# A hybrid attention block on one Trainium2 core: staged queries stored over ScalarE's queue, the second half's weights requested first, its norms moved beside the keys, the first norm weight spread by TensorE

## The chip, the cores and the metric

The kernel runs on one NeuronCore of a Trainium2 chip. TensorE multiplies matrices and transposes tiles (its weight loads are shown as PEld and overlap its matmuls), VectorE (DVE), ScalarE (ACT) and GpSimd (POOL) do the elementwise work, and DMA engines move data between DRAM and the on-chip memory. DMAs are issued by an instruction in some engine's own stream; in this kernel nearly all of them are issued by SyncE (SP), which does nothing else. An engine works through its instructions strictly in order: one that waits for a semaphore holds up everything behind it, DMA issues included. The metric is the device time of one execution in microseconds, given as the median of several executions; the kernel is also run once with the hardware profiler, and this one execution is what the views show.

## The reference, cut to what matters

One transformer block over 1024 tokens of width 1024, batch 1, in float32. The kernel keeps float32 accuracy.

```python
def reference(x, mem, ...):
    for l in range(DEPTH):                                   # DEPTH = 1
        x = x + _hybrid_mixer(_rms_norm(x, norm1_g[l]), w_in[l], ...)
        x = x + _memory_xattn(_rms_norm(x, norm2_g[l]), mem, ...)
        x = x + _sq_relu_mlp(_rms_norm(x, norm3_g[l]), ...)
...
    # in _hybrid_mixer; proj is 1024 tokens x 1760 columns
    proj = h @ w_in
    c_q, c_kv, k_idx, w_idx, q_nsa, kv_nsa, g_nsa = jnp.split(proj, splits, axis=-1)
    c_q = _rms_norm(c_q, dsa_cq_g)
    q_d = _rope(_rms_norm((c_q @ w_dsa_uq).reshape(B, L, DSA_HEADS, D), dsa_qn_g), pos)
    q_i = _rope((c_q @ w_idx_q).reshape(B, L, IDX_HEADS, IDX_DIM), pos)
    q_n = _rope(_rms_norm(q_nsa.reshape(B, L, NSA_HEADS, D), nsa_qn_g), pos)
    # per block of 128 queries: index scores and top 256 keys, an attention over those,
    # and compressed, selected and windowed attentions, mixed by gates; then o @ w_out
```

Three kinds of queries come out of the projection: `q_d` (kind 0, 8 heads of 64), `q_n` (kind 1, 8 heads) and `q_i` (kind 2, 8 heads, for the index scores). Kinds 0 and 1 are normalised per head and rotated; kind 2 is rotated only.

## The kernel before

**The projection** (`project`, L385) runs twice, for two halves (parts) of four tiles of 128 tokens each. Part 0 runs alone at the start. Part 1 runs as the first piece of a generator `fill` (driver, from L1224), and `together` interleaves `fill` with `attend`, the attention of the eight query blocks. The rest of `fill` is the keys and values of the memory (`memory`, L886), the output projection and memory attention of pairs of tiles (`between`, L929), and the first half of the MLP (`mlp`, L1059). What is left of the MLP follows by itself at the end (`mlp_tail`, L1117). The text order decides only which work is offered: a list scheduler then fixes the order of the instructions on each engine, so a few moved lines can reorder much.

**Each part** goes through these steps. The four tiles of `x` are normalised and transposed to xh (and xl in part 0). In part 0 this is `norm_T` (L293): a square with a row sum on ACT, a power on POOL (L238), a scaling by the norm weight `gb1` on DVE (L298), eight transposes on TensorE (`to_T`, L285), and evacuations by ACT and DVE (L289, L291, or L242 and L243). For part 1 the tiles have been normalised in place before, by `norm_ahead` (L375: square L380 on ACT, scaling L382 on DVE, with the norm weight loaded by `gain`, L353), so that part 1 begins with the transposes alone. Then `w_in` runs as chunks of columns, in the order (968,256), (0,256), (256,200)+(1736,24), (1224,256), (1480,256), then the small `w_dsa_ukv`, then (456,256), (712,256) beside the keys' preparation `k_prep` (L483), and at last the four gemms "ups" (`w_dsa_uq` and `w_idx_q`, two chunks of 256 columns each). In the part 0 of before, `norm_ahead` runs beside the ups.

**Weights** come in groups of two (KG) slabs of 128 rows. In part 0, `load_w` (L258, DMA L261 on SP) loads them and `split_w` splits them in a high and a low part (L251 on ACT, L256 on POOL or DVE). In part 1, `load_whole` (L268, DMA L272 on SP) loads them into the rings `whi` and `wlo` and they are used as plain float32. `mm` is L222-223, so all matmuls of the gemms show that line; their outputs go to the PSUM tile `psD`.

**The queries** are put aside in DRAM: `stage_q` (L426) copies each `psD` tile of 128x256 to an on-chip tile `st` (L430 on DVE for the tiles with t % 2 == part unless it is kind 1, else L432 on ACT), and after the fourth tile one DMA (L434, 512 KB, on SP) stores `st` to the DRAM tensor `qraw`. There are six such stores in each part. SP thus holds, in one order, the stores, the loads of the weights, and the loads of the queries below.

**The attention** reads queries back in `q_prep` (L586), four heads at a time: a load `qin` from `qraw` (L590, on SP, one buffer), for kinds 0 and 1 two small products of the rotation tables with the norm weight into `qtab` (L597, L598 on POOL, one buffer), the square (L600, ACT), the sum and power (L602 to L604), the scaling of `qin` (L605), the products `qta` (L606, POOL) and `qtb` (L607, DVE), the sums into the two halves of `qd` (L609 on DVE, L610 on POOL, one buffer), four transposes into `psPT` (L616), and the split into qh and ql (L242, L243). The queries are prepared 44 times, 32 of them with tables.

**The start.** `x`'s first tile is loaded first (L229, SP). `gb1`, the norm weight on all 128 partitions, is loaded by a broadcast DMA of 512 KB on ACT's queue (L392). The first weights (L261) and the other tiles (L373) follow on SP, then the tables (L199), small norm weights (L1234 to L1236), masks (L205) and the small loads of `project` into `pc` (L412 to L415, L422).

**DMA semaphores.** The DMAs issued by SP take eight semaphores in turn, so a DMA's issue also waits until the one eight before it has landed.

Of the kernel before, what the change touches and what calls it, by code (L numbers as in the profile page):

```python
# [9 lines left out]
F32 = mybir.dt.float32  # L10
# [6 lines left out]
AF = mybir.ActivationFunctionType  # L17
# [5 lines left out]
P = 128  # L23
L = 1024
DM = 1024
# [121 lines left out]
def alternate(*streams):  # L147
    streams = list(streams)
    i = 0
    while streams:  # L150
        i %= len(streams)
        w = next(streams[i], None)
        if w is None:
            streams.pop(i)
        else:
            i += 1
            yield w
# [12 lines left out]
def build(nc, tc, I, C, out):  # L170
    v, s, g, te = nc.vector, nc.scalar, nc.gpsimd, nc.tensor
    ctx = ExitStack()
    W = {n: I[n][0] for n in I}
# [12 lines left out]
    def pst(tag, shape):  # L186
        return psum["pool"].tile(shape, F32, tag=tag, name="ps" + tag, bufs=psum["n"][tag],
                                 padded_shape=[P, 512 // int(np.prod(shape[2:]))] + list(shape[2:]))
# [5 lines left out]
    def row(ap):  # L194
        return ap[None, :]
# [26 lines left out]
    def mm(o, a, b, start, stop):  # L222
        te.matmul(o, a, b, start=start, stop=stop)  # L223

    def small(pool, tag, w, dt=F32, bufs=2, p=P):
        return pool.tile([p, w], dt, tag=tag, name=tag, bufs=bufs)
# [66 lines left out]
    def norm_T(pool, x_t, gb, xs):  # L293
        ss = small(at, "nss", 1)
        xn = ring(pool, "x4", [P, DM])
        s.activation(xn, x_t, AF.Square, accum_out=ss)
        r = rsqrt_of(at, ss, DM, 1, "n")
        v.scalar_tensor_tensor(xn, x_t, r[:, 0:1], gb, op0=ALU.mult, op1=ALU.mult)  # L298
        to_T(pool, xn, xs, DM // P)
# [70 lines left out]
    ahead = {0: late["x"]}  # L370
# [4 lines left out]
    def norm_ahead(pool):  # L375

        gb = gain(pool, W["norm1_g"])
        for t in range(4, 8):
            ss = small(at, "nss", 1)
            s.activation(ring(pool, "x4", [P, DM]), ahead[t], AF.Square, accum_out=ss)  # L380
            r = rsqrt_of(at, ss, DM, 1, "n")
            v.scalar_tensor_tensor(ahead[t], ahead[t], r[:, 0:1], gb, op0=ALU.mult, op1=ALU.mult)  # L382
            yield 1.0

    def project(pool, part, late, st):  # L385
        t0, nt = PARTS[part]
        whole = part > 0
        _, xf, xt_of = xT(pool, nt, whole)
        begun = []
        if not whole:  # L390
            gb1 = ring(pool, "x4", [P, DM])
            s.dma_start(gb1, row(W["norm1_g"]).to_broadcast([P, DM]))  # L392
            ws = weights(pool, xf, DM // P, W["w_in"], [(968, 256)])
            for t in range(1, nt):
                begun += [next(ws) for _ in range(KG)]
                ahead[t] = small(srow, "S", L, bufs=NS)
                load_x(ahead[t], t)
            begun += list(ws)
        for t in range(nt):
            if whole:  # L400
                to_T(pool, ahead.pop(t0 + t), xt_of(t), DM // P, True)
            else:
                norm_T(pool, ahead.pop(t), gb1, xt_of(t))
            yield 1.0
        pe = late["pe"]
        cq = [ring(pool, "c8", [P, nt, 2, P], F32 if whole else F32R) for _ in xf]
# [17 lines left out]
        qst = []  # L424

        def stage_q(k, c, t, pt):  # L426
            if t == 0:
                qst[:] = [ring(pool, "st", [P, nt, 256])]
            if k != 1 and t % 2 == part:
                v.tensor_copy(qst[0][:, t, :], pt)  # L430
            else:
                s.activation(qst[0][:, t, :], pt, AF.Copy)  # L432
            if t == nt - 1:
                nc.sync.dma_start(qraw[k][part][c], qst[0])  # L434

        def consume(ci, t, pt):
            T = t0 + t
# [38 lines left out]
        def w_in(chunks, first, begun=None):  # L476
            return gemm(pool, xf, DM // P, nt, W["w_in"], chunks,
                        lambda ci, t, pt: consume(ci + first, t, pt), begun)
# [36 lines left out]
        for kv in range(0 if part else 2):  # L515
# [6 lines left out]
        yield from (alternate if part == 0 else chain)(*pair_)  # L522
        yield from gemm(pool, [lambda t, k, c=c: c[:, t, :] for c in ckv], 1, nt,
                        W["w_dsa_ukv"], [[(0, 128)]], consume_kv)
        yield from alternate(w_in([[(456, 256)], [(712, 256)]], 2), k_prep())
        ups = chain(*[gemm(pool, [lambda t, k, c=c: c[:, t, k, :] for c in cq], 2, nt,
                           W[name], [[(0, 256)], [(256, 256)]],
                           lambda ci, t, pt, k=k: stage_q(k, ci, t, pt)) for k, name in ((0, "w_dsa_uq"), (2, "w_idx_q"))])
        yield from ups if whole else alternate(ups, norm_ahead(pool))

    def compress(pool, part, KT, pe, st, ctab):
        t0, nt = PARTS[part]
# [52 lines left out]

    def q_prep(aw, t, kind, hg):  # L586

        q = small(aw, "qin", 256, bufs=1).rearrange("p (h d) -> p h d", d=64)
        part = part_of(t)
        nc.sync.dma_start(q, qraw[kind][part][hg][:, t - PARTS[part][0], :].rearrange("p (h d) -> p h d", d=64))  # L590
        ta = small(aw, "qta", 256, bufs=1).rearrange("p (h d) -> p h d", d=64)
        tb = small(aw, "qtb", 256, bufs=1).rearrange("p (h d) -> p h d", d=64)
        if kind == 2:
            A, B = cos[:, t, None, None, :].to_broadcast([P, 4, 2, 32]), sin[:, t, :]
        else:
            tab = small(aw, "qtab", 128, bufs=1).rearrange("p (a d) -> p a d", d=64)
            g.tensor_tensor(halves(tab[:, 0, :]), halves(qg[:, kind, :]), cos[:, t, None, :].to_broadcast([P, 2, 32]), op=ALU.mult)  # L597
            g.tensor_tensor(tab[:, 1, :], sin[:, t, :], qgs[:, kind, :], op=ALU.mult)  # L598
            A, B = halves(tab[:, 0, :])[:, None, :, :].to_broadcast([P, 4, 2, 32]), tab[:, 1, :]
            s.activation(ta, q, AF.Square)  # L600
            ss, r = small(aw, "qss", 4), small(aw, "qr", 4)
            v.tensor_reduce(ss, ta, axis=AX.X, op=ALU.add)  # L602
            g.tensor_scalar(ss, ss, 64 * EPS, None, op0=ALU.add)
            g.tensor_tensor(r, ss, mhalf[:, 0:1].to_broadcast([P, 4]), op=ALU.pow)  # L604
            g.tensor_tensor(q, q, r[:, :, None].to_broadcast([P, 4, 64]), op=ALU.mult)  # L605
        g.tensor_tensor(halves(ta), halves(q), A, op=ALU.mult)  # L606
        v.tensor_tensor(halves(tb), swap(q), halves(B)[:, None, :, :].to_broadcast([P, 4, 2, 32]), op=ALU.mult)  # L607
        qd = small(aw, "qd", 512, bufs=1).rearrange("p (h b d) -> p h b d", h=4, b=2)
        v.tensor_tensor(qd[:, :, 0, :], ta, tb, op=ALU.add)  # L609
        g.tensor_tensor(qd[:, :, 1, :], ta, tb, op=ALU.add)  # L610
        own = ("iqh", "iql", 1) if kind == 2 else ("qh", "ql", 2)
        qh = aw.tile([P, 4, P], F32R, tag=own[0], name=own[0], bufs=own[2])
        ql = aw.tile([P, 4, P], F32R, tag=own[1], name=own[1], bufs=own[2])
        p2 = pst("PT", [P, 4, P])
        for h in range(4):
            te.transpose(p2[:, h, :], qd[:, h, :, :].rearrange("p b d -> p (b d)"), ident)  # L616
        split_ps(p2, qh, ql)
        return qh, ql
# [633 lines left out]
    aw = aw_pool.__enter__()  # L1252
# [63 lines left out]
```

## Time and profile before

| | |
|---|---|
| median of 3 runs | 1768.23 us (1766.14 to 1768.61) |
| the profiled execution, its own time | 1767.5 us |
| its span in the profile | 1765.7 us |
| mean granted TensorE clock | 0.987 |
| TensorE busy | 1682.6 us, 95% of the span, 9326 matmuls |
| ACT, DVE, POOL busy | 1077.3, 953.5, 883.2 us |
| DMA | 188.03 MB, mean 106 GB/s |
| stores of staged queries (L434) | 12 of 512 KB, 2.9 us each from issue to landing |

How to read it: the span starts with the first instruction of the program, and 1.8 us of the execution lie outside it. Times in a row of the timeline are the start and the duration in us, then the engine, the line of the kernel, the operation, the tile written, the tiles read, the shape and the count; a bracket at the end gives the engine's idle time just before and what ended it. "SPq" marks time of SP's queue, waits included. A row of the waits gives the waiting engine and line, what released it, and then the total us, the number of waits and the longest one. A row of the windows gives for each engine the busy us and the count of instructions, then the TensorE clock that was granted, the share of the DMA engines' time, and GB/s. A row of the chain of waits gives the start, the duration and the work that the end waited for. In the groups and waits, L223 stands for every gemm and every attention matmul; the tile tells them apart.

### The profile page before, as it was taken

Reading aid. Unit: us, or ns where it says so; the run is one execution under the profiler, and the core shown is the slowest. Engines: PE = TensorE matmul, PEld = TensorE weight load, DVE = VectorE, ACT = ScalarE, POOL = GpSimd, SP = SyncE. Lnnn points to the kernel's source line nnn. Section 1 sums busy time; section 2 is a strip of 40 time slices with the busy share of each in tenths; the row PEclk is TensorE's granted clock in tenths of the full one; section 3 lists DMA queues with packets and bytes.
Section 4 is the critical chain, followed back from the end, with each engine's and each line's share of the span. In section 5 each row is a group of like instructions: output and inputs, shape, how many; then the busy total and the mean of one; then the engine's idle time right before and its main releaser. Section 6 shows DMA issues by size and latency. Waiting matters only on the chain.

```text
span 1765.7 us, 28018 instructions
## 1 busy us (share of the span) xinstructions
PE 1682.6 (95%) x9326; PEld 1446.5 (82%) x9326; DVE 953.5 (54%) x2398; ACT 1077.3 (61%) x2697; POOL 883.2 (50%) x1025
## 2 busy tenths in 40 slices
PE   6998999899998899999999999999999989999998
PEld 6997987788787778868888788888888978888887
DVE  4564668667774776545664556567645532222233
ACT  5443895995698558955599655897634533333333
POOL 2355465664442256757666667562313524444455
PEclk9998999999999899999999999999999989999999
DMA  7434312663343321222222212226257522333333
GB/s 204 128 122 115 80 51 86 205 172 111 95 146 108 96 60 58 77 77 70 65 67 70 88 59 65 66 95 202 78 187 230 162 66 89 95 96 95 96 120 108
DMA packets 173233, 188.03 MB, mean 106 GB/s; under 512 B 25248, under 2 KB 141728, under 8 KB 173088
## 3 DMA queue, kind: packets, MB, share of 16 engines
q1 hardware_dynamic: 165008, 175.22, 32.7%
q0 software_dynamic: 7936, 10.49, 2.2%
q8 instruction: 74, 1.21, 0.3%
q10 hardware_dynamic: 144, 0.52, 0.1%
q14 instruction: 71, 0.58, 0.1%
HBM read 168.36 MB, written 17.83 MB: 105 GB/s over the span
## 4 chain that ended last, share of the span: by engine, by line
PE 75%; DVE 7%; DMA 5%; ACT 5%; issue 4%; POOL 4%; SPq 1%; POOLq 0%; DVEq 0%; ACTq 0%
PE psD L223 54%; PE psS L223 8%; PE psPV L223 5%; PE psPT L729 4%; PE psM L285 1%; POOL wlo L256 1%; DMA wraw<-in_w_ff_in_dram 1%; PE psPT L616 1%; ACT dmask L670 1%; ACT S L714 1%; DVE S L712 1%; DVE pl L243 1%; POOL S L719 1%; DVE isc L644 0%; DMA whi<-in_w_out_dram 0%
## 5 line engine op out<-in xcount | busy, mean ns | idle before, releaser
L256 POOL TENSOR_TENSOR wlo<-wraw,whi 128x512 fp32r<-128x512 f32 (+1 forms) x225 | 306.8, 1369 | 289.8 <-ACT whi L251 287.8
L223 PE MATMUL psD<-whi,h 128*128 128x512 f32 x1024 | 338.6, 399 | 8.8 <-DVE b L1184 5.4
L251 ACT ACTIVATE whi<-wraw 128x512 fp32r<-128x512 f32 x321 | 200.3, 628 | 216.9 <-PE psD L223 157.4
L223 PEld LDWEIGHTS psD<-whi,h 128*128 128x128 f32 x1024 | 191.4, 189 | 54.1 <-DVE b L1184 8.8
L223 PE MATMUL psD<-xh,whi 128*128 128x512 f32 (+1 forms) x576 | 213.6, 374 | 0.9 <-ACT xh L242 0.7
L223 PE MATMUL psD<-xh,wlo 128*128 128x512 f32 (+1 forms) x576 | 213.2, 370 | 0.3 <-POOL wlo L256 0.3
L223 PE MATMUL psD<-xl,whi 128*128 128x512 f32 (+1 forms) x576 | 211.8, 369 | 0.0
L223 PE MATMUL psD<-wlo,h 128*128 128x512 f32 x512 | 203.2, 398 | 2.1 <-POOL wlo L256 2.0
L243 DVE TENSOR_TENSOR pl<-psPT,ph 128x512 fp32r<-128x512 f32 (+1 forms) x232 | 142.0, 620 | 69.1 <-ACT ph L242 67.4
L714 ACT ACTIVATE S<-S,mn 128x128 f32<-128x128 f32 (+7 forms) x192 | 142.7, 744 | 46.0 <-DVE mn L712 41.9
L223 PE MATMUL psD<-wlo,xh 128*128 128x256 f32 (+1 forms) x608 | 165.0, 348 | 0.8 <-DMA wlo<-in_w_in_dram 0.8
L223 PE MATMUL psD<-whi,xh 128*128 128x256 f32 (+1 forms) x608 | 163.3, 346 | 0.9 <-DVE Vd L243 0.9
L256 DVE TENSOR_TENSOR wlo<-wraw,whi 128x512 fp32r<-128x512 f32 (+1 forms) x96 | 78.9, 822 | 146.6 <-ACT whi L251 146.3
L242 ACT ACTIVATE ph<-psPT 128x512 fp32r<-128x512 f32 (+1 forms) x232 | 122.6, 540 | 52.7 <-PE psPT L729 45.9
L719 POOL TENSOR_SCALAR S<-S,sums,gi 128x640 f32<-128x640 f32 (+7 forms) x128 | 106.3, 839 | 87.8 <-DVE sums L717 66.1
L729 PE MATMUL psPT<-c_ident,S 128*128 128x128 f32 x816 | 131.3, 276 | 4.4 <-POOL S L719 4.0
L223 PEld LDWEIGHTS psD<-xh,wlo 128*128 128x128 f32 x576 | 108.8, 189 | 18.5 <-POOL wlo L256 1.6
L223 PEld LDWEIGHTS psD<-xh,whi 128*128 128x128 f32 x576 | 108.7, 189 | 18.2 <-ACT xh L242 1.1
L223 PEld LDWEIGHTS psD<-xl,whi 128*128 128x128 f32 x576 | 108.5, 189 | 17.4
L223 PEld LDWEIGHTS psD<-wlo,xh 128*128 128x128 f32 x608 | 114.2, 193 | 9.4 <-issue 0.9
L223 PEld LDWEIGHTS psD<-whi,xh 128*128 128x128 f32 x608 | 113.0, 192 | 9.5 <-DVE Vd L243 1.1
L223 PEld LDWEIGHTS psD<-wlo,h 128*128 128x128 f32 x512 | 96.5, 189 | 22.8 <-POOL wlo L256 5.0
(302 smaller groups left out, 3946.4 us busy)
## 6 DMA issues: line engine op xcount, KB each, us to landing
wraw<-in_w_ff_in_dram SPq DMA_DIRECT2D x40, 512.0 KB, 4.0
wraw<-in_w_ff_out_dram SPq DMA_DIRECT2D x40, 512.0 KB, 3.8
wraw<-in_w_ff_in_dram SPq DMA_DIRECT2D x64, 256.0 KB, 2.8
wraw<-in_w_ff_out_dram SPq DMA_DIRECT2D x64, 256.0 KB, 2.6
whi<-in_w_out_dram SPq DMA_DIRECT2D x32, 256.0 KB, 4.1
wlo<-in_w_out_dram SPq DMA_DIRECT2D x32, 256.0 KB, 4.1
wraw<-in_w_in_dram SPq DMA_DIRECT2D x24, 256.0 KB, 3.8
q<-st SPq DMA_DIRECT2D x12, 512.0 KB, 2.9
```

The lines of the kernel that those rows point to most:

```text
L223: te.matmul(o, a, b, start=start, stop=stop)
L242: s.activation(hi, src, AF.Copy)
L243: v.tensor_tensor(lo, src, hi, op=ALU.subtract)
L251: s.activation(hi, raw, AF.Copy)
L256: (v if l == "v" else g).tensor_tensor(lo, raw, hi, op=ALU.subtract)
L285: te.transpose(pt[:, j, :], x_t[:, (c + j) * P:(c + j + 1) * P], ident)
L616: te.transpose(p2[:, h, :], qd[:, h, :, :].rearrange("p b d -> p (b d)"), ident)
L670: s.activation(mask, src, AF.Sign, bias=c, accum_out=over)
L712: v.tensor_tensor_reduce(out=dst, in0=sp, in1=m, scale=1.0, scalar=mn[:, 0:1] if i else 3e38, op0=ALU.add, op1=ALU.min, accum_out=low)
L714: s.activation(S, S, AF.Exp, bias=low, scale=-1.0, accum_out=sums[:, hh:hh + 1])
L719: g.tensor_scalar(Ss[hh], Ss[hh], sums[:, hh:hh + 1], 1.0 if gate is None else gate[:, hh:hh + 1], op0=ALU.mult, op1=ALU.mult)
L729: te.transpose(p2[:, j, hh, :], S[:, (c + j) * P:(c + j + 1) * P], ident)
```

## The change

Six edits, all in `project` and `q_prep`:

1. The first norm weight is loaded as one row of 4 KB into partition 0 of `gb1` (still on ACT's queue); two matmuls with a row of ones as the stationary operand spread it over 128 partitions into two `psD` tiles of 128x512, and one copy on ACT and one on DVE put them into `gb1`. `norm_T`'s instructions are issued after both copies.
2. In part 1, the first chunk of `w_in` is requested at the head of the generator, ahead of the transposes.
3. `stage_q` stores over ACT's queue in place of SP's, and in both parts it is the even tiles that DVE copies.
4. `norm_ahead` runs beside the chunks (456,256), (712,256) and `k_prep` of part 0.
5. `q_prep`'s `qin` has two buffers (the default of `small`) in place of one, and the rotation tables lie in the first quarter of `qd` in place of a buffer of their own.
6. The ups of part 0 run without `norm_ahead` beside them.

```diff
-        begun = []
+        begun = list(weights(pool, xf, DM // P, W["w_in"], [(968, 256)])) if whole else []
         if not whole:
             gb1 = ring(pool, "x4", [P, DM])
-            s.dma_start(gb1, row(W["norm1_g"]).to_broadcast([P, DM]))
+            s.dma_start(gb1[0:1], row(W["norm1_g"]))
+            ones = pool.tile([1, P], F32, tag="ones", name="ones")
+            v.memset(ones, 1.0)
+            spread = []
+            for c in range(2):
+                spread.append(pst("D", [P, 512]))
+                mm(spread[c], ones, gb1[0:1, c * 512:(c + 1) * 512], True, True)
+            copies = [s.activation(gb1[:, 0:512], spread[0], AF.Copy), v.tensor_copy(gb1[:, 512:], spread[1])]
...
-                norm_T(pool, ahead.pop(t), gb1, xt_of(t))
+                with tc.issue_after(copies[0].ins), tc.issue_after(copies[1].ins):
+                    norm_T(pool, ahead.pop(t), gb1, xt_of(t))
...
-            if k != 1 and t % 2 == part:
+            if k != 1 and t % 2 == 0:
                 v.tensor_copy(qst[0][:, t, :], pt)
             else:
                 s.activation(qst[0][:, t, :], pt, AF.Copy)
             if t == nt - 1:
-                nc.sync.dma_start(qraw[k][part][c], qst[0])
+                s.dma_start(qraw[k][part][c], qst[0])
...
-        yield from alternate(w_in([[(456, 256)], [(712, 256)]], 2), k_prep())
+        yield from alternate(w_in([[(456, 256)], [(712, 256)]], 2), k_prep(), *([] if whole else [norm_ahead(pool)]))
...
-        yield from ups if whole else alternate(ups, norm_ahead(pool))
+        yield from ups
...
-        q = small(aw, "qin", 256, bufs=1).rearrange("p (h d) -> p h d", d=64)
+        q = small(aw, "qin", 256).rearrange("p (h d) -> p h d", d=64)
...
+        qd = small(aw, "qd", 512, bufs=1).rearrange("p (h b d) -> p h b d", h=4, b=2)
...
-            tab = small(aw, "qtab", 128, bufs=1).rearrange("p (a d) -> p a d", d=64)
+            tab = qd[:, 0, :, :]
...
-        qd = small(aw, "qd", 512, bufs=1).rearrange("p (h b d) -> p h b d", h=4, b=2)
```

## The prediction

> **What bounds the kernel now.** I read the page's engine totals first, then its chain, then the windows by stage, and only then the timelines of the stages with idle TensorE.
>
> ```profile
> PE 1682.6 (95%) x9326; PEld 1446.5 (82%) x9326; DVE 953.5 (54%) x2398; ACT 1077.3 (61%) x2697; POOL 883.2 (50%) x1025
> PE 75%; DVE 7%; DMA 5%; ACT 5%; issue 4%; POOL 4%; SPq 1%; POOLq 0%; DVEq 0%; ACTq 0%
> ```
>
> The first line is busy time by engine, the second the chain of waits by engine. TensorE works 95% of the span of 1765.7 us. The edits add two matmuls and take none away, so time can come only from the other 83 us (1765.7 - 1682.6) and from stretches where TensorE ran at a lower clock. The windows say where these lie:
>
> ```profile
> 0.00:25.00 25.00, 12.77 (x85) 11.62 (x86) 12.61 (x24) 12.12 (x21) 4.85 (x10) 1.00 0.67 217
> 75.00:100.00 25.00, 24.05 (x202) 23.87 (x201) 8.92 (x21) 10.01 (x31) 11.47 (x10) 1.00 0.55 179
> 100.00:125.00 25.00, 24.85 (x208) 24.54 (x208) 20.41 (x35) 13.87 (x32) 16.39 (x19) 1.00 0.39 146
> ...
> 130.00:140.00 10.00, 2.71 (x10) 1.91 (x11) 4.71 (x10) 1.99 (x4) 5.59 (x9) 0.71 0.61 147
> 140.00:150.00 10.00, 10.00 (x42) 8.51 (x41) 2.58 (x10) 2.53 (x8) 5.62 (x10) 0.78 0.96 228
> ...
> 310.00:335.00 25.00, 19.59 (x117) 15.53 (x118) 18.59 (x66) 23.12 (x74) 14.78 (x26) 1.00 0.68 218
> ...
> 500.00:650.00 150.00, 133.57 (x762) 116.64 (x760) 97.00 (x272) 108.55 (x286) 51.28 (x71) 0.94 0.36 106
> 650.00:1300.00 650.00, 637.89 (x3434) 537.62 (x3435) 384.43 (x920) 472.93 (x1073) 386.98 (x404) 1.00 0.27 82
> ```
>
> Four places are idle and lie near the edits: the start (12 us of the first 25), the seam between part 0 and part 1 (7.3 us of 130 to 140, with a granted clock of 0.71 and then 0.78), the seam between part 1 and the memory (5.4 us of 310 to 335), and the attention (16.4 us of 500 to 650, 12.1 of 650 to 1300). The seam at 130 is where three of the edits point, so I read it closely. TensorE there:
>
> ```profile
> 125.19 0.28 PE L223 MATMUL psD<-whi,c 128*128 128x256 f32 x1
> ...
> 128.53 1.04 PE L285 MATMUL psD<-c_ident,S 128*128 128x128 f32 x8
> 132.00 0.66 PE L285 MATMUL psM<-c_ident,S 128*128 128x128 f32 x4 [2.43 <-ACT xh L289]
> 136.44 1.11 PE L616 MATMUL psPT<-c_ident,qd 128*128 128x128 f32 x4 [3.79 <-POOL qd L610]
> ...
> 139.48 3.75 PE L223 MATMUL psD<-wlo,xh 128*128 128x256 f32 x8 [0.82 <-DMA wlo<-in_w_in_dram]
> ...
> 143.52 1.54 PE L223 MATMUL psD<-whi,xh 128*128 128x256 f32 x4
> ...
> 150.84 1.03 PE L223 MATMUL psD<-wlo,xh 128*128 128x256 f32 x4
> ```
>
> The ups end at 125.3. Part 1's first projection matmul starts at 139.48. Between stand only the transposes of `x` and one `q_prep`. Why the weights are late is in SP's queue, and why the transposes are late is on ACT:
>
> ```profile
> 117.00 10.76 SPq L434 DMA_DIRECT2D q<-st  x4
> 127.87 0.37 SPq L590 DMA_DIRECT2D qin<-q  x1
> ...
> 135.34 0.33 SPq L590 DMA_DIRECT2D qin<-q  x1
> 135.71 0.43 SPq L272 DMA_DIRECT2D wlo<-in_w_in_dram  x1
> ```
>
> ```profile
> 131.04 0.42 ACT L600 ACTIVATE qta<-qin 128x256 f32<-128x256 f32 x1 [3.62 <-DMA qin<-q]
> 131.36 0.58 ACT L289 ACTIVATE xh<-psM 128x512 f32<-128x512 f32 x1
> ```
>
> SP stood in the last stores until 127.8, then issued the first `qin`, the small `pc` loads, a second `qin` that had to wait for the single buffer, and only then, at 135.71, the weights. They took what the chain shows:
>
> ```profile
> 129.68 3.75 DMA pc<-in_c_ccos_dram
> ...
> 135.71 3.64 DMA wlo<-in_w_in_dram
> ```
>
> And ACT evacuated a transposed tile at 131.36 only after the square of a `qin` that it had awaited for 3.62 us. So the seam is a queue that is in the wrong order, with no work that takes the time.
>
> **The change part by part.**
>
> *The seam.* In the changed program's instruction lists, SP issues part 1's first four weight loads ahead of every `qin` and of the `pc` loads, and the stores are gone from its queue. What these loads still wait for is a ring slot (the fourth square, L380, near 117.5 by my count) and eight DMAs back (a store of part 0). I take their issue as 118 to 119, so with 3.64 us they land by 123, before the ups end. TensorE then has 32 transposes. Eight take 1.04, one more 0.11 to 0.13, so 32 take 3.5 us; their eight evacuations of about 0.6 us on two engines are shorter than that, and no `qin` square stands ahead of them on ACT any more. 125.3 + 3.5 + 0.2 gives a restart at **129.0** in place of 139.48: -10.5. The four transposes of the first `q_prep` and one score matmul, which stood inside the hole, now come after it: +0.7. Sum **-9.8**; bounds -10.5, if they find other gaps, and -6, if the last transposes wait for evacuations as they do now at 132.00 (2.43 and a second such).
>
> *The clock.* After the hole, TensorE ran a four-matmul group of 128x256 in 1.54 us (143.52), and later the same in 1.03 (150.84). By starts, the first eight take 0.40 each and the later ones 0.215. Twelve matmuls at 0.18 more give **-2.2** if the clock stays up. In the new seam the longest gap that I expect is 2.6 us, in the old one the gaps add to 7.3 within ten; bounds -2.8 and 0. [...]
>
> *The first `q_prep` of part 1's time.* Its `qtb` stands on DVE behind the `pc` tables (L416, L417), which wait for ccos. That load was issued at 129.68 and landed 3.75 later; without the stores ahead it is issued only little earlier, since `pc` loads still follow two `qin`s, the second of which waits for the store of the last queries. I estimate `qd` at 135. TensorE has 16 projection matmuls from 129.0 (16 by 0.215 = 3.4 us at full clock), so it can stand still up to 2.6 us: I take **+1.5**, bounds 0 and +2.6.
>
> *The stores on ACT.* Twelve issues on ACT's stream, by the row of L434 in SP's queue:
>
> ```profile
> L434 SPq DMA_DIRECT2D q<-st x12: 319/327/421, 100.7 to 314.7; - x12
> ```
>
> Twelve by 0.33 are 4.0 us of ACT, six of them (2.0) in a window where ACT works 13.87 of 25. Each issue stands behind the copy of the fourth tile, which ACT itself makes (the even tiles are DVE's), so what it awaits is an eviction one tile older. Behind it on ACT stand the evacuations of the next tiles, and in part 1 the attention's exponentials. TensorE pays only where `psD` is not free in time, and now that is
>
> ```profile
> PE psD L223 <- DVE st L430: 1.9, 2, 1.3
> ...
> PE psPT L616 <- POOL qd L610: 3.8, 1, 3.8
> ```
>
> 1.9 us in all for the first. I take **0**, bounds -1.9 (the waits go) and +2 (each of six issues in part 1 costs its 0.33). [...]
>
> *The seam to the memory.* The same queue is late there:
>
> ```profile
> 306.73 4.92 DMA q<-st
> ...
> 321.17 4.42 DMA whi<-in_w_xk_dram
> ```
>
> The chain runs over a store whose buffer was awaited and then over `w_xk`, requested only after SP's last store. Of the 5.4 idle us in 310 to 335 about half belongs to these two (the rest ends on DVE and ACT). I take **-2.5**, bounds -5 and 0.
>
> *Norms beside the keys.* Four squares and scalings move from the ups to 75 to 110:
>
> ```profile
> L380 ACT ACTIVATE x<-S x4: 1046/1051/1059, 116.0 to 120.1; 128x1024 f32<-128x1024 f32 x4
> ...
> L382 DVE SCALAR_TENSOR_TENSOR S<-S,nr,x x4: 1279/1284/1383, 119.4 to 125.3; 128x1024 f32<-128x1024 f32 x4
> ```
>
> 4.2 us on ACT and 5.1 on DVE. The window 75 to 100 has 15 and 16 us free on these two, and they hide it; if a scaling falls between a `psD` tile and its eviction, TensorE waits up to 1.28. **0**, bounds 0 and +2.
>
> *The first norm weight.* The timeline of the start:
>
> ```profile
> 0.72 0.41 ACTq L392 DMA_DIRECT2D x<-in_norm_g_dram  x1
> ...
> 6.07 1.06 ACT L296 ACTIVATE x<-x 128x1024 f32<-128x1024 f32 x1 [3.63 <-DMA x<-in_x_dram]
> ...
> 10.41 1.97 PE L285 MATMUL psM<-c_ident,x 128*128 128x128 f32 x8 [10.41 <-DVE nms L236]
> ```
>
> The first tile of `x` lands near 6.0 while 512 KB of `gb1` travel beside it. At the window's 217 GB/s, 512 KB are 2.4 us, so all loads of the start may land 1 to 2.4 us earlier. Against this, ACT now does a weight split and the copy of `gb1` (about 0.6 each) before the first square, DVE has the other copy, and in the new order DVE's casts of the masks and the small tables stand ahead of some of the xl subtractions and of scalings: DVE would wait for loads that land late. I trace the first transposes to 10.0 and the later ones to no gain: **0**, bounds -1.5 and +2.
>
> *`qin`, `qd` and the middle.* Two `qin` buffers let SP request queries earlier; tables in `qd` make POOL's two products wait until the previous transposes have read it. These are
>
> ```profile
> POOL qd L610 <- PE psPT L616: 54.4, 20, 10.8
> ```
>
> ```profile
> L597 POOL TENSOR_TENSOR qtab<-qg,c_cos x32: 312/319/771, 123.1 to 1154.0; 128x64 f32<-128x64 f32 x32
> ```
>
> ```profile
> L606 POOL TENSOR_TENSOR qta<-qin,qtab x32: 723/924/2013, 134.1 to 1187.5; 128x256 f32<-128x256 f32 x32
> ```
>
> POOL waited 20 times for TensorE to have read `qd`, after it had made tables and `qta`. Now these come behind the wait: 2 by 0.32 of tables and 0.92 of `qta`, about 1.5 us more from one set of transposes to the next. TensorE waited for `qd` only once (3.8 us, the seam). So the attention has slack there, and I take **0**. The reshuffle of the orders from 150 to 1300 has no better price than its idle time of 31 and 12 us in the two stretches to 1300: bounds -6 and +8. The last fifth of each engine's order is unchanged.
>
> Sum: -9.8 - 2.2 + 1.5 - 2.5 = **-13.0**. The profiled execution gives 1767.5 - 13.0 = 1754.5; the median of the runs is 0.7 above the profiled one, so **1755**.
>
> **The rivals.**
>
> *Half a seam.* The weights come early, but TensorE then stands for the next thing: the `pc` tables and the second chunk's weights, which on SP follow `qin`s that wait for the previous `q_prep`. For it: `qd` at about 135 is late either way, and the row at 130 to 140 has DMA at only 0.61, so nothing hurries. Against: the four tiles of the first chunk give TensorE 32 matmuls of 0.215, 7 us, that need no more than the first weights. Gain about half: 6 of 13, less a lower clock, and no gain at the memory: -4, so **1764**.
>
> *The middle gains too.* If two `qin` buffers take away half of the 16.4 idle us between 500 and 650 and its clock of 0.94 returns, another 10: **1745**. For it: SP's queue is in order and `qin` blocks other loads. Against: TensorE never waits for `qin`.
>
> *Slower: tables in `qd`.* Each of the 20 waits puts 1.5 us on the path from one transposes' end to the next `qd`. If attention runs along the chain `qd`, transposes, scores, softmax, as its idle time suggests, TensorE pays: all 20 cost 30, three quarters 24 with the memory seam's 2.5 lost too: -13 + 24 + 2.5 = +13.5, **1782**. It is slower than before once about 9 of 20 are exposed (9 by 1.5 = 13.5). Against: one single wait of TensorE for `qd` in 44.
>
> *Eaten.* What the seam gives, the attention takes back: part 1's fill ends 13 us earlier, and if the end is set by the chain of the attention in the middle, not by TensorE's work, the gain is idle time there: **1768**. Against: TensorE is 98% busy from 650 to 1300 (637.89 of 650).
>
> **How the numbers follow.** Forecast 1755 with 0.62, its own range 1746 to 1762 from the bounds of the seam, clock, start and memory, which don't all go one way; half a seam 0.13; the middle gains 0.09; tables in `qd` 0.09; eaten 0.07. The range leaves out the slower rival and the far ends of the others: 1741 to 1769. A difference under 0.2%, 3.5 us, is about what a measurement of this kernel can't tell from no change. Faster: 0.62 + 0.09 + 0.10 of half a seam = 0.81. Same: 0.03 + 0.06 = 0.09. Slower: 0.09 + 0.01 = 0.10.
>
> **What would show it.** Right: in the new profile the first projection matmul of part 1 starts within 4 us of the last up, no window from 120 to 160 has a clock under 0.95, and the wait `PE psPT L616 <- POOL qd L610` at the seam is under 2.6. The start's first transposes come at 9.5 to 10.5 and part 0 ends near 125. `w_xk` is requested without a store ahead, and 310 to 335 has 22 busy or more. Wrong: TensorE waits for `qd` in many rows, or SP shows L590 in front of L272 at the seam, or 500 to 1300 has over 34 us idle.

## The result and the profile after

The changed kernel takes 1776.03 us (median of 9 runs, 1774.2 to 1783.93) against 1767.09 for the kernel before (median of 9): ratio 1.0049, 95% interval 1.0034 to 1.0064. That is some 9 us slower, where 13 us faster was forecast. The profiled execution is the slowest of the nine (1783.93, span 1782.1), so places and causes are read from its trace, and sizes from the ratios. All ratios below leave out one execution of 7097.92 us, of the kernel with edits 2 and 3 alone.

The page of the changed kernel, engine totals and chain:

```profile
PE 1696.7 (95%) x9330; PEld 1458.3 (82%) x9330; DVE 953.4 (53%) x2400; ACT 1074.0 (60%) x2698; POOL 882.6 (50%) x1025
PE 52%; ACT 7%; DVE 5%; issue 3%; DMA 2%; POOL 2%; SPq 0%; ACTq 0%; POOLq 0%; DVEq 0%
```

TensorE is busy 14 us longer with four matmul records more, which are the spread of the norm weight (3.75 us). The rest is matmuls that ran longer: of the 16.4 us by which this execution's span is longer, only 2.3 are idle time. The windows of the places shown for the kernel before:

```profile
0.00:25.00 25.00, 14.78 (x68) 11.05 (x68) 10.93 (x24) 10.98 (x19) 6.71 (x10) 1.00 0.60 192
...
100.00:125.00 25.00, 23.05 (x189) 22.32 (x187) 20.33 (x31) 13.29 (x29) 20.52 (x18) 1.00 0.24 85
130.00:140.00 10.00, 8.03 (x49) 7.47 (x48) 4.24 (x13) 3.35 (x7) 0.27 (x1) 0.83 0.52 179
140.00:150.00 10.00, 10.00 (x52) 8.85 (x51) 3.67 (x8) 2.94 (x7) 7.16 (x9) 1.00 0.72 187
...
310.00:335.00 25.00, 19.05 (x84) 16.31 (x85) 16.80 (x54) 20.87 (x64) 13.38 (x25) 0.66 0.63 206
500.00:650.00 150.00, 134.82 (x759) 118.67 (x757) 92.26 (x261) 110.83 (x294) 49.94 (x71) 0.94 0.34 109
650.00:1300.00 650.00, 630.95 (x3347) 529.29 (x3348) 381.39 (x908) 463.74 (x1059) 387.42 (x405) 0.99 0.24 77
```

The hole at 130 is nearly closed: 8.03 busy in place of 2.71, and the clock is back at 1.00 from 140 to 150, in place of 0.78. 100 to 125 lost 1.8 us of busy time, though. 310 to 335 runs at 0.66 in place of 1.00, with nearly the same idle time, and 650 to 1300 does 3347 matmul records where the kernel before did 3434; 500 to 650 is as it was. The seam from TensorE's side, then ACT's side, then SP's queue:

```profile
130.70 0.28 PE L223 MATMUL psD<-whi,c 128*128 128x256 f32 x1
132.96 1.12 PE L285 MATMUL psD<-c_ident,S 128*128 128x128 f32 x4 [1.97 <-ACT st L440]
...
138.25 1.07 PE L223 MATMUL psD<-wlo,xh 128*128 128x256 f32 x4
```

```profile
122.64 0.33 ACTq L442 DMA_DIRECT2D q<-st  x1
123.01 1.07 ACT L380 ACTIVATE x<-S 128x1024 f32<-128x1024 f32 x1 [3.56 <-DVE st L438]
...
132.52 0.66 ACT L440 ACTIVATE st<-psD 128x256 f32<-128x256 f32 x2 [3.99 <-DMA q<-st]
```

```profile
124.19 0.37 SPq L272 DMA_DIRECT2D wlo<-in_w_in_dram  x1
...
126.20 8.79 SPq L598 DMA_DIRECT2D qin<-q  x2
```

The weights are requested at 124.19 in place of 135.71, as wanted. But the ups end at about 130.8 in place of 125.3, and the first projection matmul starts at 138.25 in place of 139.48. ACT stood still 3.56 us behind a store that awaited a DVE copy, and 3.99 us for a store to land.

To follow where time is gained and lost although the order of the work differs, I gave each matmul of the timelines the time that its shape usually takes from start to start, added these up along each trace, and compared the times at which two kernels reach the same sum. This **lag** (in us, plus is later than before) is worked out, not a row of a view, and good to a few us, since it moves with the usual times that are chosen. For the changed kernel it is +2.0 at 80 us of the kernel before, +4.6 at 120, -2.8 at 160, +2 at 317, +4 at 525, +9 from 660 to 950, +12 at 1040, +17 at 1265, and from there to the end between 16 and 20. So the head lost 4.6, the seam gained 7.4, and some 19 were lost between 160 and 1270, in the stages that interleave attention with the other work. One of those places, in SP's queue and on TensorE:

```profile
1190.23 9.68 SPq L1121 DMA_DIRECT2D out_dram<-b  x3
...
1211.08 0.46 SPq L272 DMA_DIRECT2D whi<-in_w_out_dram  x1
```

```profile
1219.90 2.47 PE L223 MATMUL psD<-whi,b 128*128 128x256 f32 x5 [4.44 <-DMA wlo<-in_w_out_dram]
```

The same place in the kernel before, SP and then TensorE:

```profile
1197.73 0.38 SPq L272 DMA_DIRECT2D whi<-in_w_out_dram  x1
...
1202.71 1.97 PE L223 MATMUL psD<-whi,b 128*128 128x256 f32 x8 [0.50 <-DMA whi<-in_w_out_dram]
```

SP stands in stores of the MLP's output, `w_out` is requested 13 us later than before, and TensorE waits 4.44 for it in place of 0.50. The clock at and behind this wait is lower than the 1.00 that the kernel before has in every ten microseconds from 1190 to 1230:

```profile
1210.00:1220.00 10.00, 5.54 (x33) 4.03 (x31) 6.31 (x19) 8.09 (x19) 3.51 (x5) 0.92 1.04 339
1220.00:1230.00 10.00, 10.00 (x41) 8.67 (x42) 2.35 (x11) 5.12 (x15) 1.73 (x2) 0.74 0.63 208
```

No edit touches this place. Whether it is a consequence of the buffers, or of the order that the scheduler chose, is what the experiments had to tell.

### The profile page after: what moved, and what is told of

Its sections match the earlier page's. It is cut to its first block, busy times and chain, and to the rows that moved or that the text cites. A ratio compares the mean times of both kernels' runs of the same rounds, so it can differ in the third digit from the quotient of the medians.

```text
span 1782.1 us, 28011 instructions
## 1 busy us (share of the span) xinstructions
PE 1696.7 (95%) x9330; PEld 1458.3 (82%) x9330; DVE 953.4 (53%) x2400; ACT 1074.0 (60%) x2698; POOL 882.6 (50%) x1025
## 4 chain that ended last, share of the span: by engine, by line
PE 52%; ACT 7%; DVE 5%; issue 3%; DMA 2%; POOL 2%; SPq 0%; ACTq 0%; POOLq 0%; DVEq 0%
PE psD L223 37%; PE psS L223 7%; PE psPV L223 3%; PE psPT L737 2%; ACT dmask L678 2%; POOL wlo L256 1%; ACT whi L251 1%; ACT S L722 1%; ACT ph L242 1%; PE psM L285 1%; DMA wraw<-in_w_ff_in_dram 1%; DMA wraw<-in_w_ff_out_dram 1%; ACT tkt L680 0%; DVE pl L243 0%; ACT tks L679 0%
```

## The experiments

Theory A: each edit has a price of its own at its own place, and the attention's loss is POOL's wait for `qd` ahead of the tables (the rival "tables in `qd`" of the prediction). Theory B: the attention's loss is the order that the list scheduler chooses once anything is moved, and not a wait in the new buffers. All ratios are to the kernel before, run on the same chip.

| kernel | median us | ratio (95% interval) |
|---|---|---|
| edit 1 alone | 1771.28 | 1.0010 (0.9999 to 1.0021) |
| edits 2 and 3 alone | 1762.84 | 0.9962 (0.9946 to 0.9978) |
| edits 4 and 6 alone | 1770.97 | 1.0016 (1.0005 to 1.0028) |
| edit 5 alone | 1781.69 | 1.0074 (1.0056 to 1.0092) |
| tables in `qd` alone | 1796.22 | 1.0154 (1.0141 to 1.0167) |
| two `qin` alone | 1778.02 | 1.0058 (1.0036 to 1.0080) |
| changed kernel without edit 5 | 1771.31 | 1.0014 (1.0006 to 1.0023) |
| edit 2 alone | 1770.54 | 1.0009 (0.9997 to 1.0020) |
| before, in the order of "tables in `qd`" | 1789.95 | 1.0111 (1.0091 to 1.0131) |
| changed, tables in a buffer of their own, in its order | 1780.64 | 1.0058 (1.0039 to 1.0078) |
| parity of the copies alone | 1771.32 | 1.0010 (0.9999 to 1.0020) |
| edits 2 and 3 without the parity | 1762.94 | 0.9962 (0.9948 to 0.9975) |
| edits 2, 3, 4, 6 | 1774.09 | 1.0007 (0.9993 to 1.0021) |
| edits 1, 2, 3 | 1766.31 | 0.9973 (0.9962 to 0.9984) |
| edit 3 alone | 1769.95 | 0.9988 (0.9974 to 1.0002) |

**One edit at a time.** Four kernels, each the kernel before with one group of edits, as in the diff of the change.

Edit 1 alone (`gb1` as a row, spread by two matmuls):

> The kernel before with edit 1 alone (the first norm weight as a row, spread by two matmuls). Theory A (the loss has places: the start loses about 2 us, because the spread ends only at 6.9 us and ACT squares the first tile later than before, and DVE's small casts stand ahead of an xl subtraction): +2 us, about 1769, visible before 25 us and constant behind that. Theory B (any edit of the head reorders the attention, and the loss lies there): the start's 2 us and a few us more or less between 150 and 1300.

About +2 us, with an interval that just reaches none. Its lag is +1.3 at 58 us and between -4 and +2 after that: the start's loss and no other. The start of the changed kernel shows where, on TensorE and on ACT:

```profile
3.19 3.75 PE L223 MATMUL psD<-x,ones 1*128 1x512 f32 x4 [3.19 <-DMA x<-in_norm_g_dram]
11.34 2.91 PE L285 MATMUL psM<-c_ident,x 128*128 128x128 f32 x12 [4.41 <-DVE x L298]
...
17.44 1.12 PE L285 MATMUL psM<-c_ident,x 128*128 128x128 f32 x4 [1.94 <-DVE xl L243]
```

```profile
7.22 0.58 ACT L399 ACTIVATE x<-psD 128x512 f32<-128x512 f32 x1
7.70 1.05 ACT L296 ACTIVATE x<-x 128x1024 f32<-128x1024 f32 x1
```

The spread takes 3.75 us, and the first square starts at 7.70 in place of 6.07, behind the copy that it is ordered after (7.22). The first transposes come at 11.34 in place of 10.41.

Edits 2 and 3 alone (weights first, stores on ACT's queue):

> The kernel before with edits 2 and 3 alone (part 1's first weights requested first, stores on ACT's queue, even tiles to DVE). Theory A: the seam gains what the changed kernel gained there, about 7 us from the end of the ups to 160 us, and nothing is lost later, so about 1760. Theory B: the gain is there at 160 us and is given back in the attention, so 1765 to 1770. A third reading, that the stores on ACT hold up evacuations: the ups of part 0 end 1 to 3 us later than the 125.3 of before.

0.38% faster, 6.7 us by the ratio and 5.3 by the medians. That is theory A's number for the seam, nearly whole.

Edits 4 and 6 alone (norms beside the keys):

> The kernel before with edits 4 and 6 alone (the second half's norms beside the keys). Theory A: the norms' scalings on DVE delay evictions in the ups, 1 to 3 us lost by the end of part 0, and the seam's transposes start at once, which brings nothing since the weights are late anyway: about 1768 to 1770. Theory B: no change at the seam, and a reordering of the attention of unknown sign.

+3 us. Its lag is +4.9 already at 120 us: the ups end at 129.9. In the ups a DVE copy of `st` stands behind a scaling, here on DVE and then on TensorE, which waits for the copy:

```profile
118.25 1.88 DVE L382 SCALAR_TENSOR_TENSOR S<-S,nr,x 128x1024 f32<-128x1024 f32 x1
120.16 1.04 DVE L508 TENSOR_TENSOR K<-psM,K 64x512 fp32r<-64x512 f32 x2
121.23 0.42 DVE L430 COPY st<-psD 128x256 f32<-128x256 f32 x1
```

```profile
121.71 0.39 PE L223 MATMUL psD<-whi,c 128*128 128x256 f32 x1 [1.64 <-DVE st L430]
```

Its seam, in windows, is as bad as that of the kernel before, and later:

```profile
120.00:130.00 10.00, 8.36 (x68) 8.08 (x68) 8.07 (x16) 2.80 (x7) 4.41 (x6) 1.00 0.35 139
130.00:140.00 10.00, 4.42 (x35) 3.73 (x34) 4.89 (x14) 2.97 (x6) 4.20 (x7) 0.87 0.51 136
140.00:150.00 10.00, 8.40 (x31) 6.75 (x30) 4.06 (x13) 2.38 (x7) 5.44 (x9) 0.61 1.05 276
```

Edit 5 alone (two `qin`, tables in `qd`):

> The kernel before with edit 5 alone (two qin buffers, tables in qd). Theory A with the tables at fault (the loss of the attention comes from tables in qd, which put two POOL products and qta behind the previous transposes): +8 to +12 us, about 1777, all of it between 160 and 1300. Theory B (the loss comes from the reordering and not from the tables): within 4 us of 1767.

+13.5 us against the shared runs of before, between 160 and 1270 by the lag (+1.8 at 220, +10 at 495, +9 at 870, +17 at 1267). This is a little above theory A's +8 to +12. TensorE never waits for `qd` more than the kernel before did (once, 3.6 us).

**Edit 5 in halves.** The tables alone, and the second `qin` alone:

```diff
# tables in qd alone
-            tab = small(aw, "qtab", 128, bufs=1)...
+            tab = qd[:, 0, :, :]
# two qin alone; qgs is left out for its room
-        q = small(aw, "qin", 256, bufs=1)...
+        q = small(aw, "qin", 256)...
-            g.tensor_tensor(tab[:, 1, :], sin[:, t, :], qgs[:, kind, :], op=ALU.mult)
+            g.tensor_tensor(halves(tab[:, 1, :]), halves(sin[:, t, :]), halves(qg[:, kind, :])[:, ::-1, :], op=ALU.mult)
```

> The kernel before with half of edit 5: the tables lie in qd, qin keeps its one buffer. Edit 5 whole cost 13 us. Theory A (the tables at fault: POOL cannot begin a preparation until TensorE has read the previous one): +9 to +13, about 1778. Theory B (two qin buffers at fault: queries are requested earlier on SP and stand in front of other loads): 0 to +3. Theory C (neither, but the order of the attention that comes out): a few us of either sign, and not the whole cost in one half.

> The kernel before with the other half of edit 5: two qin buffers, the tables in a buffer of their own; the room for it comes from qgs, the swapped copy of the small norm weights, which is left out and read as a swapped view instead (one small copy less on DVE at the start, the same products). Theory A (tables at fault): -3 to +2, about 1767. Theory B (two qin buffers at fault): +9 to +13, about 1778. Theory C (the order that comes out): a few us of either sign.

+28 and +10, and both together +13.5. No sum of two prices gives that: this was the first sign against theory A. The lag shows steps at few places. The largest in the first of these kernels is about +15 between 1288 and 1317 us, where the kernel before loses nothing:

```profile
1310.00:1320.00 10.00, 6.28 (x34) 4.83 (x33) 5.19 (x16) 4.58 (x13) 2.82 (x5) 0.91 1.01 307
1320.00:1330.00 10.00, 6.76 (x27) 5.89 (x27) 0.85 (x2) 0.39 (x1) 0.00 (x0) 0.67 0.68 198
1330.00:1340.00 10.00, 10.00 (x37) 8.34 (x36) 0.85 (x2) 0.39 (x1) 0.00 (x0) 0.74 0.67 223
```

No query is being prepared there any more (the last table is made at 1219). TensorE waits for `w_out`, at a clock of 0.67. The request stands on SP behind sixteen loads of the attention's outputs. A row of the waits, then SP's queue:

```profile
PE psS L223 <- DMA whi<-in_w_out_dram: 3.2, 1, 3.2
```

```profile
1312.96 13.32 SPq L935 DMA_DIRECT2D b<-o  x16
1326.39 0.38 SPq L272 DMA_DIRECT2D whi<-in_w_out_dram  x1
```

**The order held, the waits removed.** The scheduler can be given edges that fix an engine's issue order and wait for nothing. I took the order of one kernel, engine by engine, and laid it on another that makes the same instructions with other buffers:

```diff
+    made = {i.name: i for i in nc.cur_bb.bb.instructions}
+    for names in ORDER:
+        for a, b in zip(names, names[1:]):
+            tc.add_manual_dep(made[b], a, NO_SYNC, reason="order")
```

First the buffers of the kernel before in the order of the kernel with the tables in `qd`:

> The buffers and the text of the kernel before (one qin, tables in a buffer of their own), but every engine's instructions held, by edges that fix the order of issue and wait for nothing, in exactly the order in which the kernel with the tables in qd (+28 us) has them. So the order is that kernel's and the waits for qd ahead of the tables are gone. If the waits of the tables for TensorE cost the 28 us: about 1768 to 1772. If the order that the scheduler chose around these waits costs it: about 1794 to 1796. In between, each has its share.

Ratio 1.0111 in place of 1.0154: about 20 of the 28 us stay though the tables have their buffer and no table waits for TensorE. Its lag runs beside that of the other kernel all the way (about +11 against +10 at 1035, +24 against +27 at 1317). The windows of the same three stretches:

```profile
1310.00:1320.00 10.00, 7.19 (x37) 6.00 (x35) 4.14 (x12) 3.82 (x11) 2.06 (x4) 0.77 0.99 306
1320.00:1330.00 10.00, 7.48 (x25) 5.92 (x25) 0.42 (x1) 0.38 (x1) 0.00 (x0) 0.67 0.60 169
1330.00:1340.00 10.00, 10.00 (x44) 8.54 (x43) 1.70 (x4) 0.39 (x1) 0.00 (x0) 0.88 0.80 260
```

The same hole with the same clock, 0.67 from 1320 to 1330. The order makes it. The difference of the two, 0.4% or 7 to 8 us, is what the tables' wait itself costs in that order.

But this order is in part the buffer's doing. In the kernel before, POOL makes the next preparation's tables between `qta` and the second half of `qd`, in 28 of 32 cases; one of them:

```profile
165.42 0.73 POOL L606 TENSOR_TENSOR qta<-qin,qtab 128x256 f32<-128x256 f32 x1
166.57 0.32 POOL L597 TENSOR_TENSOR qtab<-qg,c_cos 128x64 f32<-128x64 f32 x1 [0.42 <-DVE qtb L607]
...
172.21 1.10 POOL L610 TENSOR_TENSOR qd<-qta,qtb 128x256 f32<-128x256 f32 x1
```

With the tables in `qd`, of which there is one, that order would wait for itself, so the tables stand behind `qd` in all 32 cases, and in the held order they still do. The experiment takes away the wait for TensorE; it doesn't part the scheduler's free choice from what the buffer forces.

Then the changed kernel with the tables in a buffer of their own, in the changed kernel's order:

> The changed kernel with the tables in a buffer of their own again (the room comes from qgs, left out and read as a swapped view), every engine held in exactly the order of the changed kernel. Two qin buffers stay. If POOL's waits for qd ahead of the tables cost time in the changed kernel: 1771 or less, since edit 5 costs it about 5 us. If the order does: about 1776, as the changed kernel.

1.0058 (1.0039 to 1.0078) against 1.0049 (1.0034 to 1.0064): nothing is won. So in the changed kernel POOL's wait for `qd` ahead of the tables, 35.6 us, costs nothing that can be measured, and theory A falls for it as far as it means that wait. The other wait, 36.7 us at L618, isn't tested by this: in the held kernel it is still there, at 36.3 (L621). And the held kernel also leaves out `qgs`, whose own price wasn't measured. Two rows of the changed kernel, one of the held one:

```profile
POOL qd L618 <- PE psPT L624: 36.7, 8, 13.8
POOL qd L606 <- PE psPT L624: 35.6, 14, 16.1
```

```profile
POOL qd L621 <- PE psPT L627: 36.3, 8, 13.0
```

The wait for `w_out` near 1210 is there too, 4.1 us without any table in `qd`:

```profile
PE psD L226 <- DMA whi<-in_w_out_dram: 4.1, 1, 4.1
```

**How far a small edit moves the order.** Only the parity of the copies of part 1 (`t % 2 == 0` in place of `t % 2 == part`):

> The kernel before, with only this of edit 3: in part 1 DVE copies the even tiles of the staged queries and ACT the odd ones, in place of the other way round. The same work on the same engines, no buffer changed. If the loss in the attention comes from the order that the scheduler happens to choose, this alone can move the time by some us in either sign, in the attention and not at the copies; if the scheduler's choice matters little, within 2 us of 1768.

+1.8 us by the ratio, not clear of none. But the parity hardly moved the order: by tile and shape, TensorE's matmuls have 9035 of 9326 in one common sequence with the kernel before. With the tables in `qd` it is 7385, with two `qin` 6950. The better witness is edit 2 alone, below: 6953, and no clear loss. So not every new order is a bad one, and how far the order moves doesn't tell what it costs.

**The seam in parts.** Edit 2 alone, edit 3 alone, and the two without the parity:

> The kernel before with edit 2 alone (first weights of part 1 requested first), the stores still on SP. If SP's stores are what holds the weights, the requests still stand behind the last stores (127.8 us in the kernel before): restart near 132 to 135 in place of 139.5, and about 1764 to 1766. If the order of the requests is enough, as fast as edits 2 and 3 together, about 1763. If the gain needs the stores off the queue, no gain, 1768.

> Edit 3 alone (stores on ACT's queue, even tiles to DVE), weights of part 1 requested as before, behind two qin loads and the small norm weights. If the stores were what blocked SP: SP reaches the weights some us earlier, 1764 to 1767. If the order of the requests blocks as well, the gain is small: 1767 to 1770.

> The kernel before with the two edits that open SP's queue (weights first, stores on ACT's queue) and the copies of part 1 as they were. If the seam's gain of about 8 us is what made edits 2 and 3 together 5 us faster, 1760 to 1764 again. If 5 us were a lucky order of the attention, anywhere from 1758 to 1772.

+1.6 and -2.1, neither clear of none, and -6.7 together (1.0009, 0.9988, 0.9962). Edit 3 alone leaves the other block in SP's queue: its first projection matmul starts at 138.61, with a clock of 0.71 from 130 to 140. Edit 2 alone does open the seam, though the stores stay on SP, and loses the gain elsewhere; its restart, and then two of its windows:

```profile
132.31 1.10 PE L223 MATMUL psD<-wlo,xh 128*128 128x256 f32 x4 [1.55 <-DMA wlo<-in_w_in_dram]
```

```profile
130.00:140.00 10.00, 7.91 (x39) 6.47 (x37) 2.81 (x7) 2.17 (x5) 3.86 (x6) 1.00 0.68 203
...
1300.00:1310.00 10.00, 7.97 (x24) 6.17 (x24) 0.85 (x2) 0.77 (x2) 0.00 (x0) 0.67 0.65 195
```

Its lag is about -7 at 160 us, still -9 at 1288, and +2 at 1317: one hole in front of `w_out`, at the place where the kernel with the tables in `qd` has its largest step, takes the whole gain. No edit touches that place, no buffer was changed here, and two `qin` alone lose about 13 us there too. The profile of the last kernel shows the seam nearly as it was forecast, first on TensorE, then in windows:

```profile
125.23 0.60 PE L285 MATMUL psD<-c_ident,S 128*128 128x128 f32 x4
...
130.52 1.07 PE L223 MATMUL psD<-wlo,xh 128*128 128x256 f32 x4
```

```profile
130.00:140.00 10.00, 9.10 (x50) 7.71 (x49) 2.64 (x7) 2.92 (x6) 4.41 (x7) 1.00 0.63 185
140.00:150.00 10.00, 10.00 (x54) 8.97 (x53) 3.10 (x10) 2.04 (x8) 2.70 (x4) 1.00 0.94 212
```

The restart is at 130.52 in place of 139.48 and the clock stays at 1.00; with the parity it is at 133.44. The profiled execution's lag is -6.2 at 160 us, -3 at 467 and -2.3 at the end, so a part is given back in the attention. With and without the parity, the kernel with the seam's edits alone is the fastest of the study, faster than the kernel before and the changed one.

**The rest of the sum.** The changed kernel without edit 5, then the seam's edits with the norms, and with the spread:

> The changed kernel without edit 5 (one qin buffer, tables in qtab). If the edits add up, -5.3 of the seam, +2.9 of the norms and +2.2 of the spread give about 1768, equal to before. If the norms beside the keys help the seam's transposes once the weights are early (they no longer wait for them), 2 to 4 us less, about 1765. If edit 5 only cost because of the order that came out without the others, about 1776 as the changed kernel.

> Edits 2 and 3 (1763 us) with edits 4 and 6, the norms beside the keys. If these cost what they cost alone (+3): 1766. If they are what holds ACT in a store's wait and DVE in the norms' scaling while psD tiles wait, and so take most of the 8 us: 1769 to 1771. If they help the seam, since the transposes no longer wait for the norms: 1759 to 1762.

> Edits 2 and 3 (1763 us) with edit 1, the norm weight spread by TensorE. If it costs the 1 to 2 us of the start and nothing else: 1765. If it makes up most of the 8 us by another order of the attention: 1768 to 1771.

1.0014, 1.0007 and 0.9973. From the seam's 0.9962, the norms add 0.45% (8 us; alone they cost 0.16%) and the spread 0.11% (2 us); with both, -0.38 + 0.45 + 0.11 = +0.18% is worked out and +0.14% measured. Edit 5 adds another 0.35% (6 us; alone 0.74%) to that, which gives the changed kernel's 0.49%. The norms' 8 us are in part at their place: the lag rises from +0.3 to +5.0 between 79 and 120 us. After the seam it is about -5 at 160, and then climbs in several steps to about +9 at the end.

## Why the prediction was wrong, point by point

*The seam*: right in mechanism, and close in size where nothing disturbs it. Restart 129.0 was forecast; 130.52 was measured with edits 2 and 3 without the parity, 133.44 with it. The weights' requests came at 126.21 and 129.12 there, not at 118 to 119. Of the clock term of -2.2 the clock is right, with 1.00 in both windows. The wait for `qd` in the seam, taken as +1.5, was 0.9 in both. In the changed kernel the restart was 138.25, since the ups ended 5.5 us later and the last stores were in the way.

*The stores on ACT*: 0 failed. The store does await "an eviction one tile older", but that isn't free: in the head, the older eviction is DVE's, and DVE made it behind a norm's scaling and a copy of the keys. ACT stood 3.56 us in the store's issue, and with it the next square and evacuations. And a staging tile is written again only when its store has landed: ACT waited 3.99 us for that at the end of the ups.

*Norms beside the keys*: "0, bounds 0 and +2" failed. The windows were right that the engines had time free (8.92 and 10.01 us busy of 25 from 75 to 100), but the scheduler put the scalings beside the ups all the same, between `psD` tiles and their copies. About 5 us were lost at that place, and 8 in all on top of the seam's edits.

*The first norm weight*: 0 was forecast within -1.5 and +2, and about +2 measured. I left out the spread itself, 3.75 us on TensorE ahead of the first square.

*The seam to the memory*: -2.5 failed. The windows from 310 to 335 are no fuller (19.05 against 19.59), at a clock of 0.66. `w_xk` was requested at 322.54, against 320.00 in the kernel before. No store stood ahead of it, but SP had waited 10.9 us for a free `qin` there. Without edit 5 the request comes at 314.88, and even then the window is only 20.64 busy, at a clock of 0.80.

*The middle*: the step that failed most. I gave it 0 within -6 and +8 because TensorE hardly ever waited for `qd`, and took the bounds from the idle time. The lag of this one execution puts 19 us there, and most of it isn't idle time but a lower clock (below). The rival "tables in `qd`" had the sign, and for the tables alone even the size (+28 against 24 to 30 worked out). That size is luck: with the order held, 20 of the 28 remain without that wait, TensorE waited for `qd` no more than before, and in the changed kernel taking the wait away brings nothing. What costs there is the order of instructions with the new buffers, forced in part by the tables' place. Why that order comes out slower than the old one isn't settled: the traces show some of its places (`w_out` requested 13 us late behind stores, the hole before 1317, short holes with a low clock, 0.67 from 1320 to 1330), not the reason. The second `qin` wasn't taken out with the order held either; alone it costs 0.58%, so how much of edit 5's loss is its doing stays open.

*The clock*: I gave the granted clock a term at the seam alone. From 311 to 316, eight matmuls of 128x256 (`psD` from `wlo` and `c`) kept TensorE busy for 4.0 us at a clock of 0.50 in the changed kernel, and for 2.0 us at 1.00 in the kernel before. Summed over windows of 10 us, the clock's shortfall (10 us times one less the granted clock) is 22 us in the kernel before and 34 in the profiled execution of the changed one; from 160 to 1280 alone it is 12 and 29. The idle time is 83 us (1765.7 - 1682.6) and 85 (1782.1 - 1696.7). So in this execution most of the loss is the clock's. In the others it is less, but still the larger part: over the nine executions the mean clock is 0.983, against 0.986 over the 28 of the kernel before that were run with the first experiments, which is an estimated 30 us against 24 (the time times one less the clock), 6 of the 9 us. By the same estimate the clock makes 12 of the 28 us of the tables alone, and all of the 10 of two `qin` alone. So by this estimate a new order costs in good part through the clock; no experiment held the clock, so this is read, not tested. What makes it fall after one hole and not after another isn't shown: the windows 310 to 335 of the two kernels are nearly equally idle (5.41 and 5.95 us), at 1.00 and 0.66, but their gaps aren't the same ones.

## What to carry to other kernels

Where a scheduler orders the instructions, a change of one buffer is a change of the order of everything behind it. Price that as a term with both signs, and measure each edit alone before they are put together. When a wait grows and the time does too, hold the order and take the wait away: here that moved most of the blame from the wait to the order. Ask then what the buffer forces in that order, and price an order not by its idle time alone: in the profiled execution here the clock's shortfall grew by 12 us, the idle time by 2. A gain at one place can be lost in a single hole far away that no edit touches, as edit 2 alone showed. And a store moved to a busy engine's queue brings its waits along, 3.56 us of ACT's time at one store here: count what stands behind it.

## What the runs showed of the hardware

Two stretches of 25 us with nearly the same idle time (5.41 and 5.95 us) had a clock of 1.00 and of 0.66 (310 to 335 in the kernel before and in the changed one); the longest single gap of TensorE was 1.62 us in the one and 1.94 in the other, where it began at 309.58. In the changed kernel a TensorE wait of 4.44 us, up to 1219.90, was followed by ten microseconds at 0.74 (1220 to 1230). In the same kernel, two matmuls of one row by 512 columns in float32 (four records) took 3.75 us at the start, before anything else ran on TensorE.
